# Regrouping the SBUF pools of a transformer block so that TensorE's operands for the expert products and the query weights share one low pool

## The chip, the core and the metric

The kernel runs on one core of a Trainium2 chip as one launch. The metric is the device time of one execution in microseconds (us), median of several runs. The engines are TensorE (PE; its weight loads are shown apart as PEld), VectorE (DVE), ScalarE (ACT), GpSimd (POOL), and SyncE (SP), whose queue issues nearly all DMAs. All matrix products of the part in question are in a four-byte format (float32r); a value is split into a high and a low half, and a product is made of three matmuls (high by high, low by high, high by low).

## The reference

One transformer block on 512 tokens of width 1024: a modulated layer norm, token mixers (sparse attention and a gated unit), a residual, and then a product-key expert layer with 16384 experts, which is where the change lies:

```
qh = (xt @ w_q).reshape(PEER_TOK_BLOCK, PEER_HEADS, 2, PEER_HALF)
s = jnp.einsum('thcd,hcnd->thcn', qh, sub_keys)
s1, i1 = lax.top_k(s[:, :, 0], PEER_TOPK)
s2, i2 = lax.top_k(s[:, :, 1], PEER_TOPK)
...
eidx = jnp.take_along_axis(cidx, pos, axis=-1)
gate = jax.nn.softmax(top_s, axis=-1)
u = expert_u[eidx]
act = jax.nn.gelu(jnp.einsum('thkd,td->thk', u, xt))
w = gate * act
return jnp.einsum('thk,thkd->td', w, expert_v[eidx])
```

## The kernel before, in words

Three of the four token blocks (`DB`, 384 tokens) are treated densely: all 16384 experts, in 128 groups of 128. For a group `e`, `u_mm` forms the activations `a_ps` (24 matmuls of 384 columns, stationary operand `u_h`/`u_l`, moving operand the normalised tokens `h2T_h`/`h2T_l`); `vw_make` multiplies them by the gates and splits the result into `w_eh`/`w_el`; `v_mm` adds `w` by `v` to six accumulators `y` (18 matmuls of 512 columns, stationary operand `w_eh`/`w_el`, moving operand `v_h`/`v_l`). The fourth block (`GB`) is gathered: indirect DMAs on POOL's queue fetch one expert row per token into a ring `grow`, and DVE does the dot products (L903) and sums (L911).

The order of the program around the change: the output projection `o` (L227 to L229) with the second layer norm, which transposes each block (`tr`, L197) into `h2T`; the query product `qh` (`wq_mm`, 16 rounds of 24 matmuls of 512 columns, stationary operand `wq_h`/`wq_l`) with key scores `sc` and a top-k on DVE; `experts` and `gates`, which turn the choice into dense gates by one-hot products `g_ps` and store them (`gdram`, L979); meanwhile the first 64 groups' `a_ps` (the last 64 groups in number, stored to `gA_d`), and then the main loop, 124 steps. Its first 61 steps have one `a_ps` and one `y` group each; the later ones `y` alone, with activations read back. A scheduler places the instructions up to the main loop on the engines' queues by a time model of its own; within the main loop the written order stands.

Pools are allocated from the low end of SBUF or, with `"right"`, from the high end; a pool opened inside a `with` gives its place back. In the built program the operands of TensorE lie as follows (KiB from the start of a partition): `h2T_h` 20 to 36, `h2T_l` 68 to 84, `u_h`/`u_l` 104 to 120, `v_h`/`v_l` 132 to 148 (16 of the last groups: 104 to 120), `w_eh`/`w_el` 186 to 199, `wq_h`/`wq_l` 202 to 218. The loads that are split into them: `u_f` 92 to 104, `v_f` 120 to 132, `wq_f` 190 to 202. Earlier stages that the prediction uses: stationary operands `oT` 20 to 36, `mT_h`/`mT_l` 36 to 68, `sT` 132 to 148; moving operands `w_h`/`w_l` 100 to 132, and, for one half of the output columns of `o`, `wo_z` 192 to 208 and `wo_s` 208 to 224. In all these products the function `mm3c` gives the activations as the stationary operand and the weight as the moving one:

```
mm(acc, lhs[0][:, k, tb], w[0][:, c, 0:n], start=k == 0, stop=False)
mm(acc, lhs[0][:, k, tb], w[1][:, c, 0:n], start=False, stop=False)
mm(acc, lhs[1][:, k, tb], w[0][:, c, 0:n], start=False, stop=k == kcs - 1)
```

Of the kernel before, what the change touches and what calls it, by code (L numbers as in the profile page):

```python
# [9 lines left out]
F32 = mybir.dt.float32  # L10
F32R = mybir.dt.float32r
# [42 lines left out]
def tile_block(ctx: ExitStack, tc: tile.TileContext, io: dict, out: bass.AP, dbg=None):  # L54
# [8 lines left out]
    def pool(stack, name, bufs=1, side=None):  # L63
        return stack.enter_context(tc.tile_pool(name=name, bufs=bufs, side=side, reuse_waits="tile"))
# [681 lines left out]
    up = pool(ctx, "up", 2)  # L746
    vp = pool(ctx, "vp", 2)
# [3 lines left out]
    with ExitStack() as es:  # L751
# [4 lines left out]
        def wq_split(hc):  # L756
            w = wqp.tile([P, KC, P], F32, name="wq_f", bufs=3)
            dma(w, io["peer_wq"][hc])
            wh = wqp.tile([P, KC, P], F32R, name="wq_h")
            wl = wqp.tile([P, KC, P], F32R, name="wq_l")  # L760
            split(wh, wl, w)
            return wh, wl
# [109 lines left out]
    gp = pool(ctx, "gp", 1, "right")  # L872
    gx = {}
    gsteps = []
    for b in GB:
        G = {}
        yacc = gp.tile([P, D], F32, name=f"yacc{b}")
        gx[b] = yacc
        h2t = gp.tile([P, D], F32, name=f"h2t{b}")
        dma(h2t, h2t_d[b])  # L880

        G["idx"] = gp.tile([P, P], I32, name=f"eidx{b}")
        G["da"] = gp.tile([P, P], F32, name=f"dact{b}")
        G["gt"] = gp.tile([P, P], F32, name=f"egate{b}")
        with ExitStack() as es:
            i1, i2, gt = experts(b, pool(es, f"gex{b}", 1, "right"))
            V.scalar_tensor_tensor(G["idx"], i1, float(P), i2, op0=ALU.mult, op1=ALU.add)
            cp(G["gt"], gt)
        V.memset(yacc, 0.0)

        def fetch(n, G=G):
            if n < 2 * P and n not in G:
                t = gp.tile([P, D], F32, name="grow", bufs=GROW)
                nc.gpsimd.indirect_dma_start(  # L894
                    out=t[:, :], out_offset=None, in_=io["peer_u" if n < P else "peer_v"],
                    in_offset=bass.IndirectOffsetOnAxis(ap=G["idx"][:, n % P:n % P + 1], axis=0))
                G[n] = t

        def ustep(k, G=G, h2t=h2t):
            for n in range(k, k + GROW):  # L900
                fetch(n)
            t = G[k]
            V.scalar_tensor_tensor(t, t, 1.0, h2t, op0=ALU.mult, op1=ALU.mult, accum_out=G["da"][:, k:k + 1])  # L903

        def wstep(k, G=G):
            act(G["da"], G["da"], AF.Gelu)
            V.tensor_tensor(G["da"], G["da"], G["gt"], op=ALU.mult)

        def vstep(k, G=G, yacc=yacc):
            fetch(P + k + GROW - 1)  # L910
            V.scalar_tensor_tensor(yacc, G[P + k], G["da"][:, k:k + 1], yacc, op0=ALU.mult, op1=ALU.add)  # L911
        gsteps += [(ustep, k) for k in range(P)] + [(wstep, 0)] + [(vstep, k) for k in range(P)]


# [71 lines left out]

    gA, u_in, u_sp = {}, {}, {}
# [7 lines left out]
    def u_split(e):  # L995
        w = u_in.pop(e)
        wh = up.tile([P, KC, P], F32R, name="u_h")
        wl = up.tile([P, KC, P], F32R, name="u_l")
        split(wh, wl, w)
        u_sp[e] = wh, wl  # L1000
# [45 lines left out]
    def vw_make(e):  # L1046

        late = e >= UL and e % 4 >= 2
        vh = (up if late else vp).tile([P, D], F32R, name="v_h", tag="u_h" if late else "v_h")
        vl = (up if late else vp).tile([P, D], F32R, name="v_l", tag="u_l" if late else "v_l")  # L1050
# [4 lines left out]
        wh = vp2.tile([P, TD], F32R, name="w_eh", bufs=NT)  # L1055
        wl = vp2.tile([P, TD], F32R, name="w_el", bufs=NT)
# [195 lines left out]
```

## Time and profile before

| | |
|---|---|
| median of 3 runs | 1731.76 us (1729.93 to 1733.48) |
| profiled execution, its own time | 1734.04 us |
| span of that profile | 1732.3 us |
| PE busy | 1683.2 us, 97% |
| mean granted TensorE clock | 0.988 of full speed |
| DMA | 423.52 MB, mean 244 GB/s |

Times in rows are us from the span's start. In a timeline row the start is the first number and the duration the second; matmuls are pipelined, so the second overlaps the next one's start, and the pace of TensorE is read from the differences of starts. In brackets stands how long the engine had been idle and what ended that. A row with xN merges N instructions of a kind.

### The profile page before, as it was taken

The page shows a single profiled execution, that of the slowest core. Times are in us where ns is not written, and L with a number is a line of the kernel's source. Part 1 is how long each engine was busy: PE and PEld are TensorE (multiplying, and loading weights), DVE is VectorE, ACT ScalarE, POOL GpSimd, SP SyncE. Part 2 cuts the span into 40 slices and gives each one's busy share as a digit, 9 for nine tenths or more (in the row PEclk, how much of TensorE's full clock was granted, in tenths as well). Part 3 has the DMA queues.
Part 4 walks back from the last instruction along what each step waited for, and adds up shares of the span by engine and source line. Part 5 has one row for each costly group of instructions (what it writes and reads, how often), then busy time and mean ns, then how long its engine had stood idle before and what let it go on. Part 6 is the DMA issues. An engine that isn't in the chain of part 4 may idle for free.

```text
span 1732.3 us, 24462 instructions
## 1 busy us (share of the span) xinstructions
PE 1683.2 (97%) x9097; PEld 1441.4 (83%) x9097; DVE 1366.3 (79%) x2682; ACT 668.6 (39%) x1029; POOL 336.6 (19%) x276
## 2 busy tenths in 40 slices
PE   5999999999989999999999999999999999999997
PEld 4977666677778899999998998899998888888885
DVE  6434777758869999997865888888888888888886
ACT  4523433343342244465553333333333333333331
POOL 0000000000000000000002544544545445333300
PEclk9999999999989999999999999999999999999998
DMA  7411344434252046577688999999999989999982
GB/s 303 170 55 49 117 181 153 152 116 151 81 197 84 25 141 223 190 270 273 245 311 326 337 354 379 339 351 339 357 342 346 355 305 315 378 382 361 369 275 82
DMA packets 163854, 423.52 MB, mean 244 GB/s; under 512 B 17171, under 2 KB 83475, under 8 KB 155927
## 3 DMA queue, kind: packets, MB, share of 16 engines
q1 hardware_dynamic: 126743, 287.71, 47.0%
q0 software_dynamic: 36992, 134.25, 20.9%
q8 instruction: 71, 1.16, 0.3%
q14 instruction: 48, 0.39, 0.1%
HBM read 381.20 MB, written 40.71 MB: 244 GB/s over the span
## 4 chain that ended last, share of the span: by engine, by line
PE 92%; DVE 3%; DMA 2%; ACT 1%; issue 0%; SPq 0%; DVEq 0%; ACTq 0%
PE y L1068 31%; PE a_ps L1007 9%; PE a_ps L1006 9%; PE a_ps L1009 9%; PE gf L227 3%; PE gf L228 3%; PE gf L229 3%; PE g_ps L975 2%; PE s L513 2%; PE qh L768 2%; PE qh L767 2%; PE qh L770 2%; PE oacc L556 2%; PE g L229 1%; PE g L228 1%; PE g L227 1%
## 5 line engine op out<-in xcount | busy, mean ns | idle before, releaser
L1006 PE MATMUL a_ps<-h2T_h,u_h 128*128 128x384 f32 x1024 | 345.5, 337 | 5.6 <-ACT h2T_h L87 4.5
L1007 PE MATMUL a_ps<-h2T_l,u_h 128*128 128x384 f32 x1024 | 345.7, 338 | 0.9 <-DVE h2T_l L88 0.9
L1052 ACT CAST v_h<-v_f 128x1024 fp32r<-128x1024 f32 x128 | 134.7, 1052 | 355.1 <-PE y L1068 259.1
L894 POOL DMA_INDIRECT grow<-in_peer_u_dram,eidx x128 | 162.4, 1269 | 466.5 <-DVE grow L903 425.3
L894 POOL DMA_INDIRECT grow<-in_peer_v_dram,eidx x128 | 162.7, 1271 | 240.2 <-DVE yacc L911 214.8
L1058 DVE TENSOR_TENSOR v_l<-v_f,v_h 128x1024 fp32r<-128x1024 f32 x128 | 156.5, 1222 | 66.2 <-ACT v_h L1052 65.8
L1068 PE MATMUL y<-v_h,w_eh 128*128 128x512 f32 x768 | 203.3, 396 | 3.0 <-ACT w_eh L1057 3.0
L1068 PE MATMUL y<-v_l,w_eh 128*128 128x512 f32 x768 | 203.2, 396 | 0.0
L1068 PE MATMUL y<-v_h,w_el 128*128 128x512 f32 x768 | 203.2, 396 | 0.0
L1009 PE MATMUL a_ps<-h2T_h,u_l 128*128 128x384 f32 x1024 | 202.2, 336 | 0.0
L1006 PEld LDWEIGHTS a_ps<-h2T_h,u_h 128*128 128x128 f32 x1024 | 193.4, 189 | 9.5 <-ACT h2T_h L87 4.7
L1007 PEld LDWEIGHTS a_ps<-h2T_l,u_h 128*128 128x128 f32 x1024 | 193.3, 189 | 4.0 <-DVE h2T_l L88 1.3
L903 DVE SCALAR_TENSOR_TENSOR grow<-grow,h2t 128x1024 f32<-128x1024 f32 x128 | 153.2, 1222 | 33.1 <-DMA grow<-in_peer_u_dram,eidx 32.6
L1009 PEld LDWEIGHTS a_ps<-h2T_h,u_l 128*128 128x128 f32 x1024 | 179.2, 188 | 0.0
L87 ACT CAST u_h<-u_f 128x1024 fp32r<-128x1024 f32 x128 | 134.5, 1051 | 108.9 <-PE a_ps L1007 97.2
L1068 PEld LDWEIGHTS y<-v_h,w_el 128*128 128x128 f32 x768 | 144.7, 188 | 35.0
L1068 PEld LDWEIGHTS y<-v_l,w_eh 128*128 128x128 f32 x768 | 144.7, 188 | 35.0
L911 DVE SCALAR_TENSOR_TENSOR yacc<-grow,dact,yacc 128x1024 f32<-128x1024 f32 x128 | 163.9, 1280 | 9.7 <-DMA grow<-in_peer_v_dram,eidx 8.1
L1068 PEld LDWEIGHTS y<-v_h,w_eh 128*128 128x128 f32 x768 | 143.7, 188 | 33.2 <-ACT w_eh L1057 3.4
L88 DVE TENSOR_TENSOR u_l<-u_f,u_h 128x1024 fp32r<-128x1024 f32 x128 | 156.3, 1221 | 18.8 <-ACT u_h L87 12.6
L1010 ACT ACTIVATE gA<-a_ps 128x384 f32<-128x384 f32 x119 | 58.7, 493 | 95.9 <-PE a_ps L1009 95.1
L1057 ACT CAST w_eh<-gA 128x384 fp32r<-128x384 f32 x119 | 60.7, 511 | 69.9 <-DVE gA L1054 66.1
(309 smaller groups left out, 2565.3 us busy)
## 6 DMA issues: line engine op xcount, KB each, us to landing
u_f<-in_peer_uT_dram SPq DMA_DIRECT2D x128, 512.0 KB, 5.1
v_f<-in_peer_vT_dram SPq DMA_DIRECT2D x128, 512.0 KB, 7.4
gdram<-g_st SPq DMA_DIRECT2D x12, 2048.0 KB, 7.2
g_rd<-gdram SPq DMA_DIRECT2D x96, 256.0 KB, 7.6
ada_w<-in_w_ada_dram SPq DMA_DIRECT2D x20, 1024.0 KB, 4.8
gA_d<-gA SPq DMA_DIRECT2D x55, 192.0 KB, 3.8
gA<-gA_d SPq DMA_DIRECT2D x55, 192.0 KB, 8.1
w_f<-in_w_merge_dram SPq DMA_DIRECT2D x8, 1024.0 KB, 4.8
```

The costliest lines, as they stand in the source:

```text
L87: i = cp(hi, src)
L88: V.tensor_tensor(lo, src, hi.bitcast(F32), op=ALU.subtract)
L227: mm(acc, lhs[0][:, k, tb], w[0][:, c, 0:n], start=k == 0, stop=False)
L894: nc.gpsimd.indirect_dma_start(out=t[:, :], out_offset=None, in_=io["peer_u" if n < P else "peer_v"], in_offset=bass.IndirectOffsetOnAxis( ...
L903: V.scalar_tensor_tensor(t, t, 1.0, h2t, op0=ALU.mult, op1=ALU.mult, accum_out=G["da"][:, k:k + 1])
L911: V.scalar_tensor_tensor(yacc, G[P + k], G["da"][:, k:k + 1], yacc, op0=ALU.mult, op1=ALU.add)
L1006: mm(a, wh[:, k], h2T[0][:, k, T0:T0 + TD], start=k == 0, stop=False)
L1007: mm(a, wh[:, k], h2T[1][:, k, T0:T0 + TD], start=False, stop=False)
L1009: mm(a, wl[:, k], h2T[0][:, k, T0:T0 + TD], start=False, stop=k == KC - 1)
L1052: cp(vh, v)
L1058: V.tensor_tensor(vl, v, vh.bitcast(F32), op=ALU.subtract)
L1068: mm(yps[i][hf], w[:, i * P:(i + 1) * P], v[:, hf * 512:(hf + 1) * 512], start=e == 0 and n == 0, stop=e == P - 1 and n == 2)
```

## The change

A pool `pe` is opened low, ahead of the staging pools, with two tags of two buffers for high and low halves each. `wq_h`/`wq_l` move into it and share the buffers of `v_h`/`v_l`; `u_h`/`u_l` follow; a pool `we` behind it takes `w_eh`/`w_el`. The staging pools `up` and `vp` come above them. The gathered block's index, gate and activation tiles get a small pool of their own (`gi`), and its large tiles (`yacc`, `h2t`, the ring `grow`) are opened only after `gates`, with the code that defines its steps.

```diff
-    up = pool(ctx, "up", 2)
-    vp = pool(ctx, "vp", 2)
+    pe = pool(ctx, "pe", 2)
+    we = pool(ctx, "we", NT)
+    up = pool(ctx, "up", 3)
+    vp = pool(ctx, "vp", 3)
...
-            wh = wqp.tile([P, KC, P], F32R, name="wq_h")
-            wl = wqp.tile([P, KC, P], F32R, name="wq_l")
+            wh = pe.tile([P, KC, P], F32R, name="wq_h", tag="v_h")
+            wl = pe.tile([P, KC, P], F32R, name="wq_l", tag="v_l")
...
-    gp = pool(ctx, "gp", 1, "right")
-    gx = {}
-    gsteps = []
+    gi = pool(ctx, "gi", 1, "right")
+    gG = {}
     for b in GB:
-        G = {}
-        yacc = gp.tile([P, D], F32, name=f"yacc{b}")
-        gx[b] = yacc
-        h2t = gp.tile([P, D], F32, name=f"h2t{b}")
-        dma(h2t, h2t_d[b])
-
-        G["idx"] = gp.tile([P, P], I32, name=f"eidx{b}")
-        G["da"] = gp.tile([P, P], F32, name=f"dact{b}")
-        G["gt"] = gp.tile([P, P], F32, name=f"egate{b}")
+        G = gG[b] = {}
+        G["idx"] = gi.tile([P, P], I32, name=f"eidx{b}")
+        G["da"] = gi.tile([P, P], F32, name=f"dact{b}")
+        G["gt"] = gi.tile([P, P], F32, name=f"egate{b}")
...
+    gp = pool(ctx, "gp", 1, "right")
+    gx = {}
+    gsteps = []
+    for b in GB:
+        G = gG[b]
+        yacc = gp.tile([P, D], F32, name=f"yacc{b}")
+        gx[b] = yacc
+        h2t = gp.tile([P, D], F32, name=f"h2t{b}")
+        dma(h2t, h2t_d[b])
+        V.memset(yacc, 0.0)
...
-        wh = up.tile([P, KC, P], F32R, name="u_h")
-        wl = up.tile([P, KC, P], F32R, name="u_l")
+        wh = pe.tile([P, KC, P], F32R, name="u_h", tag="u_h")
+        wl = pe.tile([P, KC, P], F32R, name="u_l", tag="u_l")
...
-        vh = (up if late else vp).tile([P, D], F32R, name="v_h", tag="u_h" if late else "v_h")
-        vl = (up if late else vp).tile([P, D], F32R, name="v_l", tag="u_l" if late else "v_l")
+        vh = pe.tile([P, D], F32R, name="v_h", tag="u_h" if late else "v_h")
+        vl = pe.tile([P, D], F32R, name="v_l", tag="u_l" if late else "v_l")
...
-        wh = vp2.tile([P, TD], F32R, name="w_eh", bufs=NT)
-        wl = vp2.tile([P, TD], F32R, name="w_el", bufs=NT)
+        wh = we.tile([P, TD], F32R, name="w_eh")
+        wl = we.tile([P, TD], F32R, name="w_el")
```

In the built program of the change: `v_h`/`v_l` and `wq_h`/`wq_l` 92 to 108 KiB, `u_h`/`u_l` 108 to 124, `w_eh`/`w_el` 124 to 136; `u_f` 136 to 148, `v_f` 148 to 160, `wq_f` 206 to 218, `grow` 206 to 222. Numbers of buffers are the same as before.

The scheduler also orders some work anew. On PE, where the output projection ends and the query product begins, the order before was the last `o`, the transposes of block 2 (`tr`), and a group of `a_ps`:

```order
L228 MATMUL o<-w_l,mT_h 128x512
L229 MATMUL o<-w_h,mT_l 128x512
L197 MATMUL tr<-ident,xn 128x128 x8
L1006 MATMUL a_ps<-h2T_h,u_h 128x384
L1007 MATMUL a_ps<-h2T_l,u_h 128x384
```

That group is followed by the eight transposes of block 3 and a second such group; it ends, still before, in

```order
L1006 MATMUL a_ps<-h2T_h,u_h 128x384
L1007 MATMUL a_ps<-h2T_l,u_h 128x384
L1009 MATMUL a_ps<-h2T_h,u_l 128x384 x8
L767 MATMUL qh<-h2T_h,wq_h 128x512 x2
L768 MATMUL qh<-h2T_l,wq_h 128x512
```

After the change the transposes of both blocks stand together on PE and the query product follows them (line numbers are two higher there):

```order
L228 MATMUL o<-w_l,mT_h 128x512
L229 MATMUL o<-w_h,mT_l 128x512
L197 MATMUL tr<-ident,xn 128x128 x16
L769 MATMUL qh<-h2T_h,wq_h 128x512 x2
L770 MATMUL qh<-h2T_l,wq_h 128x512
```

So two groups of `a_ps` (48 matmuls) no longer stand ahead of the query product; they come later. The second place is SP's queue at the end of `gates`, before the main loop. Before, from the last store of gates (`gdram_5094`) to the read of block 2's gates from the same tensor (`g_rd`):

```order
L979 DMA gdram_5094<-g_st 128x4096
L1023 DMA gA_d<-gA 128x384
L993 DMA u_f<-in_peer_uT_dram 128x1024
L1023 DMA gA_d<-gA 128x384
L993 DMA u_f<-in_peer_uT_dram 128x1024 x2
L1044 DMA v_f<-in_peer_vT_dram 128x1024
L144 DMA rowr<-mod_d 128x1024
L94 DMA rowr<-in_ln_g_dram 128x1024
L94 DMA rowr<-in_ln_b_dram 128x1024
L1040 DMA g_rd<-gdram_5094 128x4x128
```

After the change (`gdram_5096` is the same tensor; its last store stands one row above this piece, and the load of `h2t` two rows above that store):

```order
L1047 DMA g_rd<-gdram_5095 128x4x128
L1030 DMA gA_d<-gA 128x384
L1000 DMA u_f<-in_peer_uT_dram 128x1024
L1030 DMA gA_d<-gA 128x384
L1000 DMA u_f<-in_peer_uT_dram 128x1024
L1030 DMA gA_d<-gA 128x384
L1000 DMA u_f<-in_peer_uT_dram 128x1024
L1030 DMA gA_d<-gA 128x384
L144 DMA rowr<-mod_d 128x1024
L94 DMA rowr<-in_ln_g_dram 128x1024
L94 DMA rowr<-in_ln_b_dram 128x1024
L1047 DMA g_rd<-gdram_5096 128x4x128
```

The store and the read stand earlier against the groups of `a_ps`: on PE 62.6 groups stand ahead of the last `g_ps` before and 59.5 after, and 68 ahead of the first `y` in both.

## Rows read from the trace of the kernel before

**Rows 1.** Page: busy time, and the chain that ended last, by engine.
```profile
PE 1683.2 (97%) x9097; PEld 1441.4 (83%) x9097; DVE 1366.3 (79%) x2682; ACT 668.6 (39%) x1029; POOL 336.6 (19%) x276
...
PE 92%; DVE 3%; DMA 2%; ACT 1%; issue 0%; SPq 0%; DVEq 0%; ACTq 0%
```

**Rows 2.** Busy by stretch: from:to, length, PE, PEld, DVE, ACT, POOL, clock, DMA share, GB/s.
```profile
600.00:900.00 300.00, 298.83 (x2208) 293.86 (x2208) 269.86 (x696) 153.33 (x234) 6.99 (x7) 1.00 0.64 228
...
930.00:1440.00 510.00, 510.00 (x2547) 459.43 (x2546) 433.17 (x567) 178.42 (x244) 242.70 (x193) 1.00 0.96 344
1440.00:1690.00 250.00, 250.00 (x1069) 201.04 (x1068) 213.42 (x260) 93.14 (x124) 77.82 (x59) 1.00 0.98 345
```

**Rows 3.** Busy by stretch, tile y alone: length, PE, PEld, DVE, clock, DMA, GB/s.
```profile
1470.00:1690.00 220.00, 220.00 (x941) 176.92 (x940) 0.00 (x0) 1.00 0.99 353
```

**Rows 4.** Timeline of PE in o: 24 matmuls with high, then 24 with low operands.
```profile
439.50 0.40 PE L227 MATMUL o<-wo_s,mT_h 128*128 128x512 f32 x1
...
445.11 0.40 PE L227 MATMUL o<-w_h,mT_h 128*128 128x512 f32 x1
...
447.19 0.39 PE L227 MATMUL o<-w_h,mT_h 128*128 128x512 f32 x1
...
450.59 0.40 PE L227 MATMUL o<-wo_s,mT_h 128*128 128x512 f32 x1
```

**Rows 5.** Timeline of PE in br, stationary operand sT: 1st and 17th of a run.
```profile
411.88 0.39 PE L228 MATMUL br<-w_l,sT 128*128 128x512 f32 x1
...
415.51 0.39 PE L229 MATMUL br<-w_h,sT 128*128 128x512 f32 x1
```

**Rows 6.** Timeline of PE, main loop: 1st and 9th a_ps behind y, next y.
```profile
1193.71 0.33 PE L1006 MATMUL a_ps<-h2T_h,u_h 128*128 128x384 f32 x1
...
1195.13 0.34 PE L1006 MATMUL a_ps<-h2T_h,u_h 128*128 128x384 f32 x1
...
1197.90 1.57 PE L1068 MATMUL y<-v_h,w_eh 128*128 128x512 f32 x6
```

**Rows 7.** Timeline of PE: behind two qh rounds; then 4th and 17th matmul of qh.
```profile
508.98 0.34 PE L1006 MATMUL a_ps<-h2T_h,u_h 128*128 128x384 f32 x1
...
511.79 0.39 PE L768 MATMUL qh<-h2T_l,wq_h 128*128 128x512 f32 x1
...
514.84 2.03 PE L770 MATMUL qh<-h2T_h,wq_l 128*128 128x512 f32 x8
```

**Rows 8.** Timeline, from the end of o to the query product.
```profile
481.16 0.69 PE L1006 MATMUL a_ps<-h2T_h,u_h 128*128 128x384 f32 x1 [4.47 <-ACT h2T_h L87]
...
489.62 2.90 ACT L205 ACTIVATE tr_f<-tr,modT,sc2p 128x128 f32<-128x128 f32 x8 [0.24 <-PE tr L197]
...
493.61 1.05 ACT L87 CAST wq_h<-wq_f 128x1024 fp32r<-128x1024 f32 x1 [1.08 <-DMA wq_f<-in_peer_wq_dram]
...
495.23 0.50 PE L767 MATMUL qh<-h2T_h,wq_h 128*128 128x512 f32 x1 [1.08 <-ACT h2T_h L87]
```

**Rows 9.** Busy by stretch there, columns as in rows 2.
```profile
481.00:487.00 6.00, 4.93 (x14) 4.53 (x15) 5.65 (x14) 1.02 (x3) 0.00 (x0) 0.50 0.84 255
...
497.00:501.00 4.00, 4.00 (x12) 3.15 (x11) 3.51 (x4) 0.60 (x1) 0.00 (x0) 0.57 0.74 266
```

**Rows 10.** Timeline ahead of the first y.
```profile
917.70 0.38 SPq L1040 DMA_DIRECT2D g_rd<-gdram  x1
...
928.99 1.67 PE L1068 MATMUL y<-v_h,w_eh 128*128 128x512 f32 x6 [3.05 <-ACT w_eh L1057]
```

**Rows 11.** Page, costliest groups: busy, mean ns of one, idle before and what ended it.
```profile
L1052 ACT CAST v_h<-v_f 128x1024 fp32r<-128x1024 f32 x128 | 134.7, 1052 | 355.1 <-PE y L1068 259.1
```

**Rows 12.** Waits of SP's queue, 1460 to 1660 us: sum, times, longest.
```profile
SPq L1044 <- DVE v_l L1058: 106.7, 42, 3.7
```

**Rows 13.** DMA, 1460 to 1660 us: GB/s of 40 slices; issues, us to landing.
```profile
GB/s 289 273 397 402 354 378 397 393 355 406 343 351 405 403 349 398 384 353 380 399 335 386 356 340 357 400 361 336 384 402 347 387 364 285 355 403 396 349 380 285
...
v_f<-in_peer_vT_dram SPq DMA_DIRECT2D x49, 512.0 KB, 7.4
```

More of the change, by code (lines that the diff above doesn't have):

```diff
@@ L888, in tile_block @@
             cp(G["gt"], gt)
[L889 to L912, printed above, removed]
     gdram = {b: dramp.tile([4, P, P, 32], F32, name=f"gdram{b}") for b in DB}
@@ L984, in tile_block, with fetch, ustep, wstep @@
             gates(b, gwk)
+    gp = pool(ctx, "gp", 1, "right")
[8 more added lines that the diff above has]
+        V.memset(yacc, 0.0)
+        def fetch(n, G=G):
+            if n < 2 * P and n not in G:
+                t = gp.tile([P, D], F32, name="grow", bufs=GROW)
+                nc.gpsimd.indirect_dma_start(
+                    out=t[:, :], out_offset=None, in_=io["peer_u" if n < P else "peer_v"],
+                    in_offset=bass.IndirectOffsetOnAxis(ap=G["idx"][:, n % P:n % P + 1], axis=0))
+                G[n] = t
+        def ustep(k, G=G, h2t=h2t):
+            for n in range(k, k + GROW):
+                fetch(n)
+            t = G[k]
+            V.scalar_tensor_tensor(t, t, 1.0, h2t, op0=ALU.mult, op1=ALU.mult, accum_out=G["da"][:, k:k + 1])
+        def wstep(k, G=G):
+            act(G["da"], G["da"], AF.Gelu)
+            V.tensor_tensor(G["da"], G["da"], G["gt"], op=ALU.mult)
+        def vstep(k, G=G, yacc=yacc):
+            fetch(P + k + GROW - 1)
+            V.scalar_tensor_tensor(yacc, G[P + k], G["da"][:, k:k + 1], yacc, op0=ALU.mult, op1=ALU.add)
+        gsteps += [(ustep, k) for k in range(P)] + [(wstep, 0)] + [(vstep, k) for k in range(P)]
     gA, u_in, u_sp = {}, {}, {}
```

## The prediction

> **What bounds the kernel.** I read first the page's busy times and its chain that ended last: PE is busy 97% of the span and makes 92% of the chain [rows 1]. The view by stretch says where: in the main loop (930 to 1440 us with `a_ps` and `y`, then `y` alone) PE is busy all of the time at full clock, and from 600 to 900 us nearly so [rows 2]. DVE is at 85%, DMA at 0.96 to 0.98. So time is won only where PE's own pace rises, or where one of its few gaps closes.
>
> PE's pace is read from starts, not from busy time. In the stretch with `y` alone 941 matmuls of 512 columns touch 220 us; less the two cut by its ends that is 220/939 = 234.3 ns each [rows 3]. Is that the floor? The output projection answers. Its two halves run the same code on the same stationary operands; only the moving operand lies elsewhere. With `wo_s` and `wo_z` (192 to 224 KiB) 24 matmuls take 445.11 - 439.50 = 5.61 us, 233.8 ns each; with `w_h`/`w_l` (100 to 132 KiB) the next nine take 2.08 us, 231 ns each, and the 15 behind them 3.40 us, 226.7 ns each [rows 4]. The slow pace comes with the high operand and fades over some nine matmuls once both are low. `sT`, a stationary operand at 132 to 148 KiB, allows the fast pace too: 16 starts in 3.63 us, 226.9 ns [rows 5]. `a_ps`, both operands low, shows the echo: behind a group of `y` its first eight matmuls of 384 columns take 1.42 us (177.5 ns each), the following 16 take 2.77 us (173.1 each) [rows 6]. And `qh`, with stationary `wq` at 202 to 218 KiB, keeps 13 starts in 3.05 us, 234.6 ns, to the end of its round [rows 7]. Every slow product has an operand at 186 KiB or above, every fast one both below 148. The change puts all operands of `qh` and `y` below 136.
>
> **The change, part by part.** (1) `y`: 6 x 3 x 128 = 2304 matmuls go from 234.3 to 226.7 ns: 7.6 ns x 2304 = 17.5 us. The bounds are 0 (if address is not the cause) and the full 17.5; I take the full, since in the loop they follow `a_ps`, which is at its fast pace by then, without a gap.
>
> (2) `qh`: the first two rounds are counted in (4). The other 14 follow `sc`, whose operands `keys` and `qh` stay at 198 KiB and above, so I let nine matmuls of each 24 run at 231 ns and 15 at 226.7: 9 x 3.3 + 15 x 7.6 = 0.14 us a round, 2.0 us. Bounds 0 and 24 x 7.6 x 14 = 2.6.
>
> (3) `a_ps` behind `y`: 8 x 4.4 ns = 35 ns in each of 61 groups, 2.1 us; bounds 0 and 2.1.
>
> (4) The order ahead of `qh`. Before, two `a_ps` groups fill PE while block 3 is normalised; now they come later, and the schedule behind has no hole for them (1.2 us idle of 300 [rows 2]). But they were not free there either: PE waited 4.47 us, then worked at the lower of the clock's two levels (1.2 of 2.4 GHz, 0.50 from 481 to 487 us), and `qh` started at 495.23 because ACT cast `wq_h` late, after a wait for its load, ahead of `h2T_h` [rows 8, 9]. Now the order on ACT is the eight `tr_f`, then both `h2T_h`, with two `wq_h` cast before: `tr_f` ends at 489.62 + 2.90 = 492.5, one cast of `h2T_h` (an estimate of 0.6 us, from the 1.05 us of a cast twice its size [rows 8]) gives a start at 493.1. From there 48 `qh` at 227.5 ns, an estimate between the two paces, are 10.9 us. PE idles longer before, so part runs at half clock: before, two stretches with 6.0 us at 0.50 and 4.0 us at 0.57 [rows 9], which lost 4.0 x 0.43 = 1.7 and 6.0 x 0.50 = 3.0 us; I take 2.5. Then 48 `a_ps` still owed, 8.3 us. Sum 493.1 + 10.9 + 2.5 + 8.3 = 514.8 against 508.98 with the same work done [rows 7]: a loss of 5.8 us. Bounds: a start at 492.0 and 1.7 lost, 3.9; a start as late as before and 3.0 lost, 8.4.
>
> (5) The first `y` waits 3.05 us for `w_eh`, behind gates whose read was issued 11.3 us before [rows 10]. In the new order that read stands behind the store of `gA` of the last but one of the first 64 groups; some five `a_ps` groups of 4.2 us lie between, 20 us. The wait goes: 3.0 us won, bounds 0 and 3.05. `w_e`'s own pool also spares it the wait for the place of `gates`.
>
> (6) Nothing for the rest. A cast from `wq_f` at 190 KiB takes 1.05 us and one from `v_f` at 120 KiB 1.052 [rows 8, 11], so staging at other addresses costs ACT nothing. `h2t`, `yacc` and the first four `grow` rows now come at the end of `gates`. `h2t` stands in SP's queue ahead of gate reads, a store and `u_f` loads: the three `u_f` buffers cover a delay of two groups, 8 us; without that cover it would cost up to one group, 4.2 us. The first rows have about eight `a_ps` groups, 35 us, before DVE wants them. `wq_h` in the buffers of `v_h` meets no `v_h` for 300 us.
>
> Sum: -17.5 - 2.0 - 2.1 + 5.8 - 3.0 = -18.8 us on the profiled execution's 1734.0, 1715.2. That execution is 2.3 us above the median of the runs, so I predict 1713.0 for the median. A difference of 0.2% (3.5 us) is about what a measurement here can tell from none.
>
> **Rivals.** *DMA takes over.* With `y` alone DMA share is 0.98, and 250 us of work would have to come in 3% less; the last 67 steps hold 67 x 18 x 7.6 = 9.2 us of the gain. If loads set the pace there, that is lost: 1722. For it: 345 GB/s already, 0.98 share [rows 2]. Against: SP's loads of `v_f` wait for a free buffer (42 of 49, 106.7 us in 200 [rows 12]), not for the DMA engines; a load lands in 7.4 us while three buffers give 3 x 18 x 0.2267 = 12.2, and slices reach 400 to 406 GB/s where the row's mean of 365 would have to become 377 [rows 13]. ACT too waits for PE to free `v_h`, 259.1 us [rows 11]. Chance 0.12.
>
> *Six banks.* `y` changes its accumulator with every matmul; every product that I saw settle at 226.7 stays in one for 12 or more. If that keeps it at 231 to 232, `y` gains 2.8 ns, 6.5 us, and `a_ps` nothing: -6.5 - 2.0 + 5.8 - 3.0 = -5.7, 1726. Against: at the slow pace six banks (`y`, 234.3) and one (`o`, 233.8; `qh`, 234.6) are alike [rows 3, 4, 7]. Chance 0.07.
>
> *The address is not the cause.* Then only the order acts, and one place decides: the filler lost ahead of `qh`, 5.8 us (3.9 to 8.4), of which at most 3.0 return at the first `y`: 1734.6 to 1737.6, slower by up to 0.34%. It decides once PE's gain is under 3 us. For it: paces also vary within a product, and slow ones are later in the program, where DMA is busier. Against: `o` alternates within one stretch [rows 4]. The Trainium skill speaks for this rival: its page "TensorE: Matmul & The Clock Gate", section "Back-to-back issue gap", makes the isolated gap a function of the columns alone (about 216 ns for 512 at full clock), and "SBUF — State Buffer", section "Who interferes with whom", says that PE waits for no other user of SBUF; by both, placement gives nothing. Two paces of one shape in the rows of `o` disagree with the first. Chance 0.10.
>
> *The hole is deeper.* If the first `wq_f` load comes late, because its place is that of `wo_s` until `o` ends, the ACT queue stalls ahead of `xn` and the debt doubles to some 12 us: 1719. Chance 0.05.
>
> **Numbers.** My forecast has 0.66, with its own range 1708 to 1718. DMA and the deeper hole stay below 1724; these three make 0.83, so the range is 1708 to 1724. Faster: 0.66 + 0.12 + 0.07 + 0.05 = 0.90. The last rival's 0.10 is split: same 0.05, slower 0.05.
>
> **What would show it.** In the profile after: starts of `y` 226 to 227 ns apart (about 970 matmuls in 220 us); `qh` rounds ending at that pace; `a_ps` at 173 from its first matmul; two transposes in a row, idle PE from 477 to about 493 us, low clock at the start of `qh`; no wait of the first `y`; PE still busy all through the main loop. I am wrong if `y` keeps 234 ns, if PE shows idle time behind `v_f` or `gA` loads after 1440 us, or if the query product starts after 495 us.

## The result, and the profile after

The changed kernel takes 1721.5 us (median of 6 runs, 1720.4 to 1724.7) against 1731.8 before (6 runs, 1728.2 to 1733.5): the ratio is 0.9947, with a 95% interval of 0.9936 to 0.9959. It is faster, as forecast. 1721.5 lies inside the range of 1708 to 1724, which also covers two of the rivals, but outside the forecast's own 1708 to 1718: the gain is 10.3 us where the sum said 18.8.

The two profiles are 13.6 us apart, more than the medians. A part of that lies ahead of every instruction that the change touches: from 162 to 171 us, in `gf`, the execution of before has a lower granted clock. These are the two kernels' rows of busy time by stretch, before first (columns as in rows 2):

```profile
162.00:171.00 9.00, 9.00 (x37) 6.88 (x36) 1.72 (x7) 0.89 (x2) 0.00 (x0) 0.62 0.00 0
```
```profile
162.00:171.00 9.00, 9.00 (x52) 6.52 (x49) 2.77 (x10) 2.42 (x5) 0.00 (x0) 1.00 0.00 0
```

At 0.62 instead of 1.00 fifteen matmuls fewer fit, and the last `o` matmul then starts at 474.28 us before and at 469.82 after. Of the 18 profiles of this study six start the last `o` at 473.4 to 474.4 us, and just these six have the clock of 0.62 there; the other twelve start it at 469.1 to 471.7. PE has the same order of work up to that place in all of them. Five of the six are the kernel before or made from it (of eight), one, e4, is made from the changed kernel (of ten): both sides show it, but that it is chance alone is not shown. Below I therefore count each profile from the start of its last `o` matmul to the end of its span and call that the **remainder**: 1258.1 us before, 1248.9 after, 9.2 less.

Page of the changed kernel: busy time, and the chain that ended last (answers rows 1).

```profile
PE 1661.9 (97%) x9097; PEld 1437.6 (84%) x9097; DVE 1365.8 (79%) x2682; ACT 670.9 (39%) x1029; POOL 349.7 (20%) x276
...
PE 95%; DVE 2%; ACT 1%; DMA 1%; issue 0%; SPq 0%; DVEq 0%; ACTq 0%
```

Busy by stretch of the changed kernel, columns as in rows 2, with one more row for the end of `gates`:

```profile
600.00:900.00 300.00, 299.93 (x2234) 295.61 (x2233) 264.75 (x655) 157.61 (x239) 7.01 (x7) 1.00 0.64 233
898.00:931.00 33.00, 28.46 (x152) 28.00 (x151) 13.91 (x18) 10.45 (x15) 1.74 (x2) 0.90 0.92 351
930.00:1440.00 510.00, 510.00 (x2574) 463.47 (x2573) 431.90 (x565) 179.44 (x245) 251.36 (x194) 1.00 0.96 345
1440.00:1690.00 250.00, 250.00 (x1104) 207.06 (x1103) 216.65 (x265) 96.85 (x128) 81.13 (x58) 1.00 0.97 348
```

PE is still busy through the whole main loop, and starts more matmuls in the same time: 1104 against 1069 with `y` alone, but only 2574 against 2547 beside the `a_ps`. The DMA engines carry it (348 GB/s, share 0.97); that rival did not come. The second row is new: 4.5 us of idle PE between 898 and 931 us, and a clock of 0.90, since behind that gap some `a_ps` start 320 ns apart instead of 173, at the lower level (1.2 of 2.4 GHz).

With `y` alone the pace is what was forecast, 972 matmuls in 220 us (941 in rows 3):

```profile
1470.00:1690.00 220.00, 220.00 (x972) 182.20 (x971) 0.00 (x0) 1.00 0.98 350
```

One step of the loop with `a_ps`, timeline of PE (first and ninth `a_ps` behind `y`, the three sixes of `y`, the next `a_ps`; answers rows 6):

```profile
1158.62 0.33 PE L1013 MATMUL a_ps<-h2T_h,u_h 128*128 128x384 f32 x1
...
1160.04 0.34 PE L1013 MATMUL a_ps<-h2T_h,u_h 128*128 128x384 f32 x1
...
1162.81 1.55 PE L1075 MATMUL y<-v_h,w_eh 128*128 128x512 f32 x6
1164.20 1.53 PE L1075 MATMUL y<-v_l,w_eh 128*128 128x512 f32 x6
1165.57 1.52 PE L1075 MATMUL y<-v_h,w_el 128*128 128x512 f32 x6
1166.93 0.33 PE L1013 MATMUL a_ps<-h2T_h,u_h 128*128 128x384 f32 x1
```

The first eight `a_ps` take 1.42 us and the other sixteen 2.77, to the hundredth what they took before [rows 6]: nothing was gained there. And the sixes of `y` take 1.39, 1.37 and 1.36 us, so 231.7, 228.3 and 226.7 ns a matmul: only the last is at the forecast pace.

### The profile page after: what moved, and what is told of

It is laid out like the page before. It is cut to its first block, busy times and chain, and to the rows that moved or that the text cites. A ratio compares the mean times of both kernels' runs of the same rounds, so it can differ in the third digit from the quotient of the medians.

```text
span 1718.7 us, 24472 instructions
## 1 busy us (share of the span) xinstructions
PE 1661.9 (97%) x9097; PEld 1437.6 (84%) x9097; DVE 1365.8 (79%) x2682; ACT 670.9 (39%) x1029; POOL 349.7 (20%) x276
## 4 chain that ended last, share of the span: by engine, by line
PE 95%; DVE 2%; ACT 1%; DMA 1%; issue 0%; SPq 0%; DVEq 0%; ACTq 0%
PE y L1075 30%; PE a_ps L1014 10%; PE a_ps L1013 10%; PE a_ps L1016 10%; PE gf L227 3%; PE gf L228 3%; PE gf L229 3%; PE g_ps L947 3%; PE s L513 2%; PE qh L769 2%; PE qh L770 2%; PE qh L772 2%; PE oacc L556 2%; PE g L229 1%; PE g L227 1%; PE pT L547 1%
## 5 line engine op out<-in xcount | busy, mean ns | idle before, releaser
L973 POOL DMA_INDIRECT grow<-in_peer_u_dram,eidx x128 | 168.1, 1314 | 473.9 <-DMA u_f<-in_peer_uT_dram 273.6
L973 POOL DMA_INDIRECT grow<-in_peer_v_dram,eidx x128 | 170.0, 1328 | 223.8 <-DVE yacc L990 196.6
L1075 PE MATMUL y<-v_h,w_eh 128*128 128x512 f32 x768 | 199.2, 391 | 0.0
L1016 PE MATMUL a_ps<-h2T_h,u_l 128*128 128x384 f32 x1024 | 198.6, 334 | 0.0
L1075 PE MATMUL y<-v_l,w_eh 128*128 128x512 f32 x768 | 198.2, 390 | 0.0
L1075 PE MATMUL y<-v_h,w_el 128*128 128x512 f32 x768 | 197.5, 389 | 0.0
L1075 PEld LDWEIGHTS y<-v_l,w_eh 128*128 128x128 f32 x768 | 144.2, 188 | 31.4
```

The source lines that it names most:

```text
L973: nc.gpsimd.indirect_dma_start(out=t[:, :], out_offset=None, in_=io["peer_u" if n < P else "peer_v"], in_offset=bass.IndirectOffsetOnAxis( ...
L1016: mm(a, wl[:, k], h2T[0][:, k, T0:T0 + TD], start=False, stop=k == KC - 1)
L1075: mm(yps[i][hf], w[:, i * P:(i + 1) * P], v[:, hf * 512:(hf + 1) * 512], start=e == 0 and n == 0, stop=e == P - 1 and n == 2)
```

## The experiments

The theory of the prediction was that a TensorE operand high in SBUF makes a matmul slow. All pools from the high end, however, also began at another byte: counted modulo 256 bytes, each low operand of rows 3 to 7 started at 128 and each high one at 224. The runs take the two apart. The pace is the mean distance between starts of `y` from 1500 to 1690 us; "off" is the start of `w_e` less that of `v` modulo 256; the heights and starts are those of the built program. The pace of `qh`, where it is named, is read from the second to the last matmul of a round.

| run | `w_e` at KiB | off, bytes | `y`, ns | remainder, us | time, us |
|---|---|---|---|---|---|
| before | 186 to 198 | 96 | 234.3 | 1258.1 | 1731.8 |
| changed | 124 to 136 | 0 | 226.7 | 1248.9 | 1721.5 |
| e1 staging low | 167 to 179 | 0 | 226.7 | 1249.7 | 1723.1 |
| e2 w_e high | 174 to 186 | 96 | 234.3 | 1257.1 | 1730.2 |
| e6 w_e high, pad | 174 to 186 | 64 | 233.3 | 1254.3 | 1726.0 |
| e7 low, pad 32 | 124 to 136 | 0 | 226.7 | 1247.7 | 1719.2 |
| e10 low, w_e +64 | 124 to 136 | 64 | 233.3 | 1262.9 | 1734.3 |
| e8 before, pad 32 | 186 to 198 | 64 | 233.3 | 1255.6 | 1728.3 |
| e9 before, pad 96 | 186 to 198 | 0 | 226.7 | 1239.6 | 1713.0 |
| e11 before, pad 224 | 186 to 198 | 128 | 232.4 | 1252.2 | 1723.7 |
| e13 before, pad 352 | 186 to 198 | 0 | 226.7 | 1240.5 | 1716.0 |

(Times of e8 and e9 are medians, of the other experiments in this table single runs.)

**e1: the operands above the staging buffers.**

```diff
-    pe = pool(ctx, "pe", 2)
-    we = pool(ctx, "we", NT)
     up = pool(ctx, "up", 3)
     vp = pool(ctx, "vp", 3)
     gring = pool(ctx, "gring")
+    pe = pool(ctx, "pe", 2)
+    we = pool(ctx, "we", NT)
```

> The changed kernel with the order of its pools turned round: the staging buffers (u_f, v_f, gA) at the bottom, the TensorE operands (wq, u, v halves, w_e) above them, from 135 to 179 KiB. Address theory (an operand that lies above a limit between 148 and 186 KiB slows the matmul): if the limit is above 179 KiB, the 512-column y matmuls stay at 226.7 ns in the y-only stretch and the time stays at 1720 to 1722; if it is between 148 and 179, y goes to some value up to 234.3 and the time up to about 1737. Rival (what counts is only that the operands lie together or below their staging buffers, or the order of code): y at 234.3 again, with qh (v_h, v_l at 135 to 151 KiB, which is within the bounds already seen as fast) at 234.3 as well. qh tells these apart: 228.9 by the address, 234.3 by the rival.

Nothing slows down; `qh` is at 228.9. By the theory of height a limit would have to lie above 179 KiB.

**e2: only `w_e` high.**

```diff
-    we = pool(ctx, "we", NT)
...
     vp2 = pool(ctx, "vp2", 2, "right")
+    we = pool(ctx, "we", NT, "right")
```

> The changed kernel with only w_eh and w_el put back high (behind the gate reads, on the right side), the halves of v, u and wq low as changed. Theory that any one operand above the limit slows the matmul: y at 234.3 ns everywhere, qh and a_ps as in the changed kernel, the time about 1720 + 2304 x 6.7 ns = 1736. Rival that only the moving operand (v) counts: y at 226.7 and the time 1720. Rival that each operand gives its share: y near 230.5, the time near 1728.

`y` is back at 234.3 with one operand moved. But `w_eh` at 174 to 180 KiB is as slow as `w_el` at 180 to 186 here, where e1 was fast with `w_el` up to 179: no limit of height fits both. What differs is the start byte. Busy time by stretch with `y` alone, e1 and then e2:

```profile
1470.00:1690.00 220.00, 220.00 (x972) 182.25 (x971) 0.00 (x0) 1.00 0.99 355
```
```profile
1470.00:1690.00 220.00, 220.00 (x941) 176.87 (x940) 0.00 (x0) 1.00 0.99 348
```

**e6, e7, e8: shifts that tell height from start.** Each adds one unused tile: in e6 32 bytes ahead of the high `w_e` of e2, in e7 32 bytes below `pe` in the changed kernel, in e8 32 bytes at the high end in the kernel before.

```diff
+    pool(ctx, "pad", 1, "right").tile([P, 8], F32, name="pad")
     we = pool(ctx, "we", NT, "right")
```
```diff
+    pool(ctx, "pad").tile([P, 8], F32, name="pad")
     pe = pool(ctx, "pe", 2)
```
```diff
+    pool(ctx, "pad", 1, "right").tile([P, 8], F32, name="pad")
     hp = pool(ctx, "hp")
```

> The run with w_eh and w_el high had y at 234.3 ns with them at 174.47 to 186.47 KiB, and the run with the staging low had 226.7 with them at 167.4 to 179.4 KiB. In bytes, every operand of a slow product so far starts 32 bytes past a multiple of 64, every operand of a fast one on a multiple of 64. So this is w_e high again with one unused tile of 32 bytes ahead of it: w_e at 174.44 to 186.44 KiB, on multiples of 64. Theory that the start modulo 64 bytes sets the pace: y at 226.7 in the y-only stretch, the time about 1730 - 15 = 1715. Theory of the prediction, that a high address sets it: y stays at 234.3, the time at 1730.

> The changed kernel with one unused tile of 32 bytes below its TensorE operands: all of them (halves of wq, v, u and w_e) as low as in the changed kernel, 91.9 to 135.9 KiB, but 32 bytes past a multiple of 64. Theory of the start modulo 64: y back at 234.3 ns everywhere, qh at 234.3, the time at 1737 to 1740 (2304 x 6.7 = 15.4 and 336 x 5.4 = 1.8 on 1721.5). Theory of the high address: y 226.7 and qh 228.9, the time at 1721.

> The kernel before with nothing changed but one unused tile of 32 bytes at the high end of SBUF, which shifts all that is allocated from that end, wq and w_e and the output weights among it, on multiples of 64 bytes and leaves each at its height. Theory of the start modulo 64: y at 226.7 ns in the y-only stretch and 229 beside the a_ps, qh at 228.9, and with the order of work of before (two groups ahead of qh, the first fetches early) the whole gain without the changed kernel's two losses: 15.4 + 1.9 = 17 less than before, 1714 to 1715. Theory of the high address: y at 234.3, the time that of before, 1732.

My second theory, that starts must be multiples of 64 bytes, fell in all three: with such starts `y` stays slow in e6 and e8, and without them it stays fast in e7. Height seemed to win. But e7 has a contradiction to height in it: there `qh` fell back to 233.2 ns although `wq` lies at 92 to 108 KiB. In e7 `wq` starts 32 bytes off `h2T`, while `v` and `w_e` moved together. So the third theory: what counts is that the two operands of a matmul start at the same byte modulo some power of two. e8 is 0.9993 of before (0.9983 to 1.0003), so a pad by itself is worth nothing.

**e9, e10, e11, e13: equal and unequal starts at either height.** e9, e11 and e13 are e8 with 96, 224 and 352 bytes; e10 puts 64 bytes between the halves and `w_e` in the changed kernel.

```diff
+    pool(ctx, "pad", 1, "right").tile([P, 24], F32, name="pad")
     hp = pool(ctx, "hp")
```
```diff
     pe = pool(ctx, "pe", 2)
+    pool(ctx, "pad").tile([P, 16], F32, name="pad")
     we = pool(ctx, "we", NT)
```

> The kernel before with one unused tile of 96 bytes at the high end of SBUF: w_e stays at 186.4 KiB and wq at 201.9 KiB, but both now start at the same byte modulo 128 as the operand that they are multiplied with (v, and h2T). Theory that a product is fast where its two operands start at the same byte modulo 128 and slow where they do not, whatever their height: y 226.7 in the y-only stretch and about 229 beside the a_ps, qh 228.9, the o matmuls with the first weights 4 to 7 ns faster, and 2304 x 6.7 + 336 x 5.4 = 17.2 less than before: 1713 to 1715 where before gives 1731. Theory of the high address: 234.3, no change.

> The changed kernel with one unused tile of 64 bytes between the halves of v and u and w_e: all of them low, at 91.9 to 135.9 KiB, but w_e starts 64 bytes off v modulo 128. Theory of equal starts modulo 128: y 233.3 ns everywhere, as in the run with w_e high at the same 64 bytes off, qh 228.9, the time 1721.5 + 2304 x 6 ns = 1733 to 1736. Theory of the high address: y 226.7, 1721.

> The kernel before with an unused tile of 224 bytes at the high end: w_e at 186.25 KiB and wq at 201.75, at the same byte as v and h2T modulo 128, but 128 bytes off modulo 256 and 512. If 128 is what counts: y 226.7, qh 228.9, 1714. If it is 256 or 512: y and qh at 233 to 235, 1731.

> The kernel before with an unused tile of 352 bytes at the high end: w_e and wq start at the same byte as v and h2T modulo 256, but 256 bytes off modulo 512. With 96 bytes (the same byte modulo 512) y took 226.67 ns and the time was 1713; with 224 bytes (128 off) y took 232.4. If equal starts modulo 256 are what counts: y 226.7, qh 227.1, 1713. If modulo 512: y and qh between 230 and 235, about 1722 to 1730.

Busy time by stretch with `y` alone, e9 (high, equal), e10 (low, 64 off), e11 (128 off) and e13 (256 off):

```profile
1470.00:1690.00 220.00, 220.00 (x972) 182.25 (x971) 0.43 (x1) 1.00 0.95 339
```
```profile
1470.00:1690.00 220.00, 220.00 (x945) 176.31 (x944) 0.00 (x0) 1.00 0.99 353
```
```profile
1470.00:1690.00 220.00, 220.00 (x948) 178.36 (x947) 0.00 (x0) 1.00 0.95 344
```
```profile
1470.00:1690.00 220.00, 220.00 (x973) 182.15 (x972) 0.00 (x0) 1.00 0.96 342
```

That settles it for `y`: low and unequal is slow, high and equal is fast, and 256 bytes off counts as equal. PE's order of work is that of before, matmul for matmul, in all runs made from it with unused tiles (e8, e9, e11, e13 to e16), so no reordering is behind these gains. (The 1723.7 us of e11 are below its forecast of 1731 mostly because its `o` ends early; its remainder is 5.9 us below that of before.) `qh` follows: 227.1 ns in e9 and e13, 233.3 in e8 (64 off), 232.4 in e11 (128), 234.3 before (96). The `o` products are 0.7 us shorter in e9, as `wo` now starts with `mT`, and the nine slow matmuls that stood behind `wo` [rows 4] are gone: these are the first and the tenth at the same place in e9's timeline, 2.04 us apart (226.7 ns each) instead of 2.08.

```profile
444.70 0.39 PE L227 MATMUL o<-w_h,mT_h 128*128 128x512 f32 x1
...
446.74 0.39 PE L227 MATMUL o<-w_h,mT_h 128*128 128x512 f32 x1
```

One unused tile of 96 bytes makes the kernel before 0.9896 of itself (0.9876 to 0.9917): more than the whole change.

**e3, e5: the wait at the end of `gates`.** In the changed kernel PE waits there once, 4.5 us for `u_h`. These are rows of its waits from 895 to 935 us, of PE and of ACT (sum, times, longest), and one of SP's queue in the timeline:

```profile
PE a_ps L1013 <- ACT u_h L87: 4.5, 1, 4.5
```
```profile
ACT gA L1017 <- DMA gA_d<-gA: 5.9, 1, 5.9
ACT u_h L87 <- DMA u_f<-in_peer_uT_dram: 4.9, 3, 3.5
```
```profile
890.89 7.61 SPq L1030 DMA_DIRECT2D gA_d<-gA  x1
```

The cast that PE waits for begins at 910.4 us. ACT's queue had stood until 909.2 for a store of `gA` to land, and stood 0.7 us more for `u_f` (the 3.5 are of an earlier cast). The load of that `u_f` was issued only at 898.6, since SP's queue was held for 7.6 us by the issue of a store of `gA` ahead of it; in e3 no issue of such a store between 890 and 905 us takes over 2.2. So it is not `u_f` alone that is late there, but what goes through SP's queue, stores too.

e3 fills the first four `grow` tiles by `memset`; e5 loads the `x1` rows and the three rows `gt2`, `lg`, `lb` in the loop, one in every second step.

```diff
+                if n < GROW:
+                    nc.gpsimd.memset(t, 0.0)
+                else:
                     nc.gpsimd.indirect_dma_start(
```
```diff
-    dma(xr, x1_d.rearrange("b p d -> p b d"))
-    mod_rows(gt2, 5)
-    rows(lg, io["ln2_g"])
-    rows(lb, io["ln2_b"])
...
             v_mm(e)
+            if 16 <= e < 30 and e % 2 == 0:
+                late_rows((e - 16) // 2)
```

> The changed kernel without the first four gathered rows' loads (2 MB from DRAM; GpSimd fills these four tiles with zeros instead, so this part of the gathered experts is left out). Theory that this burst, which now falls into the end of the gates, makes the u loads late: the wait of a_ps for u_h of 4.5 us at the end of the gates goes, the four groups from a_ps no. 62 to no. 66 take 18.6 us again instead of 23.4, and the time falls by 4 to 5 us to about 1716. Rival that the order on the loads' queue (h2t, the block of x1 rows and the rows of the last norm ahead of the u loads) is the cause: 23.4 us stay, and the time is 1720 to 1721.

> The changed kernel with the 3.5 MB of x1 rows and rows of the last norm loaded inside the loop over y (from its 17th to its 29th step) instead of at the end of the gates. Theory that the burst at the end of the gates (2 MB of first fetches, h2t, these rows, the reads of the gates) makes u_f late: with the larger half of it gone, the four groups from a_ps no. 62 to no. 66 take 18.6 us or less instead of 23.4, and the time falls by 5 to 7 us to about 1715. Rival that the first fetches alone stand in the way (they go on GpSimd's queue, right ahead of the u loads): less than 2 us, 1720. If the loop over y has no slack for 3.5 MB, y waits in its 17th to 29th step and the gain is given back there.

Busy time by stretch at the end of `gates`, e3 and then e5 (the changed kernel's row stands above: 28.46 busy, 0.90):

```profile
898.00:931.00 33.00, 33.00 (x186) 32.26 (x185) 15.52 (x20) 12.59 (x18) 3.93 (x3) 1.00 0.93 349
```
```profile
898.00:931.00 33.00, 32.60 (x182) 31.54 (x181) 14.81 (x19) 12.00 (x18) 3.94 (x3) 1.00 0.90 318
```

Both clear the wait (0.4 us of it stay in e5), and the clock stays at 1.00. From the 63rd `a_ps` group to the first `y` it takes 25.0 us in e3 and 25.6 in e5 against 31.8 in the changed kernel, and the remainder of e3 is 5.7 us shorter. e5 gives back 3.1 in the loop (501.3 against 498.2 us from the first `y` to the last `a_ps`), so 2 stay. My rival that the first fetches alone stand in the way is not borne out: taking other loads out of the stretch does as much.

**e4: the two groups put back in the code.** The helpers of the loop over `u` and its first two passes move ahead of the query product:

```diff
+    for i in range(2):
+        ku_step(i)
     with ExitStack() as es:
         wqp = pool(es, "wqp", 2, "right")
...
-    for i in range(KU):
+    for i in range(2, KU):
+        ku_step(i)
```

> The changed kernel with the first two a_ps groups of the loop over u put back ahead of the query product, as their order was before, nothing else. Theory that their 48 matmuls fill a hole of TensorE ahead of the first qh and so were lost there by the change: a_ps no. 55 comes 5.4 us earlier against the last o than in the changed kernel (that is 127.6 to 128.2 us behind it instead of 132.5), and the time falls by 4 to 5.5 us to 1715 to 1717. Rival that the hole is as long either way, since the clock is low in it and the norm of the last block ends it: less than 2 us, 1719 to 1721.

A miss: the ratio is 0.9932 (0.9909 to 0.9955), no different from the change's. The scheduler put the 48 `a_ps` behind 46 `qh` matmuls, so the hole stayed open. But e2 had brought the old order back by accident. Timeline of the changed kernel (the last transposes, the first `qh`, the first loads of `u_f`), then of e2:

```profile
484.16 1.97 PE L197 MATMUL tr<-ident,xn 128*128 128x128 f32 x8 [11.93 <-ACT xn L720]
...
488.83 1.22 PE L769 MATMUL qh<-h2T_h,wq_h 128*128 128x512 f32 x2 [2.70 <-ACT h2T_h L87]
...
492.62 6.94 SPq L1000 DMA_DIRECT2D u_f<-in_peer_uT_dram  x4
```
```profile
471.51 1.29 SPq L999 DMA_DIRECT2D u_f<-in_peer_uT_dram  x3
...
480.98 0.69 PE L1012 MATMUL a_ps<-h2T_h,u_h 128*128 128x384 f32 x1 [7.25 <-ACT h2T_h L87]
```

In the changed kernel `u_f` is loaded 22.8 us behind the last `o`, in e2 0.2. Its place there, 136 to 148 KiB, is that of the rows `x` of the norm (138 to 154), which are in use until the last block is normalised; without `w_e` below it, in e2, it is 124 to 136, which is free. That speaks for the addresses as the cause of the moved order, and so does e4, where the code alone did not bring the groups back. It is not the late load alone: in e1 `u_f` is loaded 3.3 us ahead of the last `o`, and the order is that of the changed kernel all the same. There `wq` lies at 135 to 151 KiB and `u` above it, so these lie on the rows `x`, and their casts come at 488.9 and 490.8 us, behind the norm of the last block. That the shared place is what the scheduler reacts to is argued from these layouts; no run moves one tile alone. Up to the 56th `a_ps` matmul (before, the first behind the whole query product) it takes 125.2 us from the last `o` in e2 and 125.5 in e6 (same order), and 132.6 in the changed kernel, with `qh` at one pace in all three: the price of the moved order is 7.1 to 7.3 us. It is known to about 1 us, since e3, e5 and e10, which have the changed kernel's order and `qh`, take 133.6 to 133.8.

**e14, e15, e16: the slow first matmuls.** In e7 the loop's `y` had been at 226.8 ns from its second matmul on, and `a_ps` at 173.6 instead of 174.5. e14 carries its offsets to the kernel before: 64 bytes at the high end, 32 below `up`, 32 ahead of `wq`. e15 has the 32 bytes above the `u` tiles instead; e16 moves `u` alone (96 bytes at the high end, 32 below `up`, 224 ahead of `vp`).

```diff
+    pool(ctx, "pad", 1, "right").tile([P, 16], F32, name="pad")
     hp = pool(ctx, "hp")
...
+    pool(ctx, "padl").tile([P, 8], F32, name="padl")
     up = pool(ctx, "up", 2)
...
+        pool(es, "padq", 1, "right").tile([P, 8], F32, name="padq")
         wqp = pool(es, "wqp", 2, "right")
```

> The kernel before with three unused tiles, 64 bytes at the high end of SBUF, 32 bytes below u_f on the low side, 32 bytes ahead of wq: v and w_e start at the same byte modulo 512, and so do h2T and wq, and u is 32 bytes past h2T, as in the two runs in which the first y matmuls behind the a_ps were not slower. Theory that this offset of u against h2T (not the height of the operands, nor the pools of the changed kernel) takes the slow first matmuls away: y 226.8 in the loop, a_ps mean 173.6 instead of 174.5 there, a loop of 494.6 instead of 499.9 us, and with the o matmuls 32 bytes off (0.5 lost) 4 to 5 us less than the run with 96 bytes: 1707 to 1710. Rival that the slow first matmuls depend on something else of those kernels: 229 and 1713.

> The run with three unused tiles, but with the 32 bytes on the low side above the u tiles instead of below them: u starts at the same byte as h2T modulo 256 again, v and w_e stay 32 bytes past it and equal to each other. (Of the last 64 groups 32 take the u tiles for v and are then 32 bytes off w_e, so they are slow here: only the loop up to 1420 us is read.) If u against h2T takes the slow first matmuls away: they are back, y 229.1 and a_ps 174.5 ns in the loop. If it is the start of v and w_e against u and h2T: y 226.8 and a_ps 173.6.

> The opposite: u 32 bytes past h2T modulo 256, v and w_e at the same byte as h2T (and, as above, 32 groups of the last 64 slow, so only the loop is read). If u against h2T takes the slow first matmuls away: y 226.8 and a_ps 173.6 ns. If it is v and w_e against u and h2T: 229.1 and 174.5, or something between when both take part.

One step of e14 in the timeline of PE, same places as above:

```profile
1160.51 0.34 PE L1009 MATMUL a_ps<-h2T_h,u_h 128*128 128x384 f32 x1
...
1161.90 0.34 PE L1009 MATMUL a_ps<-h2T_h,u_h 128*128 128x384 f32 x1
...
1164.68 1.52 PE L1071 MATMUL y<-v_h,w_eh 128*128 128x512 f32 x6
1166.04 1.52 PE L1071 MATMUL y<-v_l,w_eh 128*128 128x512 f32 x6
1167.40 1.52 PE L1071 MATMUL y<-v_h,w_el 128*128 128x512 f32 x6
1168.76 0.34 PE L1009 MATMUL a_ps<-h2T_h,u_h 128*128 128x384 f32 x1
```

All three sixes take 1.36 us, the first eight `a_ps` 1.39. `y` is at 226.8 ns in the loop of e15 and at 228.8 in that of e16: it is `v` and `w_e`, starting 32 bytes past `h2T`, that take the slow `y` away, not `u`. `a_ps` is at 173.7 and 173.5 in the two, so for it either move does. e14 took 1710.7 us, just above its forecast, 0.9893 of before (0.9877 to 0.9910), remainder 1236.8. (The last 64 groups, of which 32, not 16, take the `u` tiles for `v`, are left out of these readings.)

**e12: the readings in one kernel.** The changed kernel with 32 bytes below `pe`, `wq` back in `wqp` on the same start as `h2T`, `up` below `we`, and the `x1` rows loaded in the loop.

```diff
+    pool(ctx, "pad").tile([P, 8], F32, name="pad")
     pe = pool(ctx, "pe", 2)
-    we = pool(ctx, "we", NT)
     up = pool(ctx, "up", 3)
+    we = pool(ctx, "we", NT)
...
+        pool(es, "padr", 1, "right").tile([P, 24], F32, name="padr")
         wqp = pool(es, "wqp", 2, "right")
...
-            wh = pe.tile([P, KC, P], F32R, name="wq_h", tag="v_h")
+            wh = wqp.tile([P, KC, P], F32R, name="wq_h")
```

> A version that puts the readings together: the changed kernel with u_f below w_e in the order of the pools (it then no longer lies on the x rows of the norm before, so that the two a_ps groups go ahead of the first qh again), with u, v and w_e 32 bytes past h2T modulo 128 (as in the run in which the first matmuls after each change of width were not slower), wq back high at the same byte as h2T modulo 128, and the x1 rows (2 MB) loaded in the loop over y instead of at the end of the gates. Sum against the changed kernel's 1721.5: two groups back -5.4, no slow first matmuls in the loop -3.6, the 2 MB out of the burst -5 or so, what the loop gives back +1: 1708 to 1711, qh at 228.9 and y at 226.7 throughout. If the wait at the end of the gates comes from the first fetches alone: 1713 to 1716.

It takes 1709.4 us, 0.9879 of before (0.9857 to 0.9900): faster than both kernels, not told apart from e9 or e14. The sum came out, its parts did not, so the hit is luck. The order and `qh` gave 10.3 us (122.3 against 132.6 to the 56th `a_ps`); moving the `x1` rows gave next to nothing at the end of `gates` (31.4 us against 31.8, with other changes beside it) and the loop took 3.2 us more (497.8 against the 494.6 of e7).

## Why the prediction was partly wrong

The steps along the remainder, forecast and measured between the same places of the two profiles:

| stretch | forecast, us | measured, us |
|---|---|---|
| last `o` to 56th `a_ps`: (2) and (4) | -2.0 + 5.8 | +4.6 (128.0 to 132.6) |
| to the first `y`: (5), (6) | -3.0 | +1.1 (326.7 to 327.9) |
| loop with `a_ps`: 61 groups of (1), and (3) | -8.3 - 2.1 | -5.7 (503.9 to 498.2) |
| `y` alone: the rest of (1) | -9.2 | -9.3 (286.7 to 277.4) |
| end | 0 | +0.1 |
| sum | -18.8 | -9.2 |

The missing 9.6 us are 4.7 in the loop with `a_ps`, from (1) and (3), 4.1 from (5) and (6), and 0.8 from (2) and (4).

**(1), the size** was right with `y` alone: 226.7 ns. In the loop it was taken in full because `a_ps` "is at its fast pace by then". That step failed: the first nine `y` of a group still take 231 ns on average, so a matmul gains 5.1 ns there instead of 7.6, 2.7 us short in 61 groups. For `qh` I had counted nine slow matmuls a round; for `y` I had not.

**(1), the reason** was wrong. "Every slow product has an operand at 186 KiB or above" was true of the rows, and so was its confounder, the start byte. e10 is slow with everything low, e9 fast with `w_e` at 186 and `wq` at 202 KiB. The gain with `y` alone was therefore luck: the change worked because one chain of pools on the low side happens to give `v`, `w_e`, `wq` and `h2T` the same start modulo 256. The two paces in `o` [rows 4] are the same thing: `wo` started 96 bytes off `mT`. The rival "the address is not the cause" falls too, since it held that placement gives nothing. The Trainium skill, whose page "TensorE: Matmul & The Clock Gate", section "Back-to-back issue gap", makes the isolated gap of a matmul a function of its columns alone, spoke for it. Here 512 columns took 226.7 to 234.3 ns at full clock, and e9 against before changes nothing but start bytes, so the measurement decides against that.

**(2)** was right: 336 matmuls of `qh` went from 234.3 to 228.9 ns, 1.8 us. **(4)** was right in mechanism: with 1.8 for (2) taken out the first row leaves +6.4 for the order, where 5.8 in a range of 3.9 to 8.4 was forecast (e2 and e6 say 7.1 to 7.3).

**(3)** failed too and gave nothing of its 2.1 us: `a_ps` behind `y` kept its 1.42 us for eight. I read the slow first matmuls as an echo of the high operand ahead. They stay when all operands start on one byte (after, e1, e9, e13), and go when `u` or `v` and `w_e` are shifted by 32 (e14 to e16). A change of the number of columns is not needed for slow first matmuls: the nine in `o` [rows 4] have 512 on both sides.

**(5) and (6)** failed: the first `y` no longer waits, as forecast, but the `a_ps` ahead of it do, 4.5 us, and then run at a lower clock. (6) had named the cover, three `u_f` buffers for `h2t` in SP's queue, but looked at that queue only; the four fetches of 2 MB on POOL's queue, moved into the same 30 us as 3.5 MB of rows and the gate reads, were costed by when DVE wants them and not by what they take from SP's queue. Without them, in e3, the remainder is 5.7 us shorter.

"Six banks" is excluded: `y` settles at 226.7 with six accumulators. "The hole is deeper" is not what happened: the first `qh` started 19.0 us behind the last `o`, against 20.9 before.

**Open.** Why two starts 256 bytes apart count as equal, why `a_ps` (384 columns) keeps 173.3 ns with `u` 32 bytes off `h2T`, why a shift of 32 removes the slow first matmuls, what lets the scheduler move the two groups, and which of the loads at the end of `gates` holds SP's queue: e3 and e5 relieve it from either side, and in e12, without the `x1` rows there, PE still waits 3.7 us for `u_h`.

## What to carry to other kernels

When one matmul shape runs at two paces, list the start bytes of both operands beside their heights before giving the reason a name, and test it with an unused tile of a few bytes, which shifts the starts and leaves the heights and the order of work: 96 bytes did more here than regrouping the pools. A gain in pace that is read in a uniform stretch should be booked in full only for such stretches; where the loop alternates two shapes, read the first matmuls behind each change. And a buffer moved to another address can inherit the waits of whatever lay there, and a scheduler's program may come out in another order far from the edit. A transfer that is moved should be costed also by what it holds up in the other queues.

## What the runs showed of the hardware

- A matmul of 512 float32r columns takes 226.7 ns at full clock when both operands start on the same byte modulo 256, and 233.2 (32 bytes off, `qh` of e7), 233.3 (64), 234.3 (96) and 232.4 ns (128) when not, with the operands anywhere between 20 and 218 KiB.
- With `h2T`, `u`, `v` and `w_e` all on one start, the first nine `y` behind `a_ps` average 231 ns and the first eight `a_ps` behind `y` some 177 (173.3 for the others); with `v` and `w_e` 32 bytes further these `y` take 226.8.
- In the changed kernel a wait of 4.5 us of PE, up to 911.5 us, is followed by `a_ps` at a lower granted clock (0.90 over 898 to 931 us, 1.00 in e3 without the wait). From the 63rd group to the first `y` it takes 6.8 us longer than in e3, not 4.5.
